# Even attention of a two-layer transformer: ScalarE's and VectorE's orders chained beside TensorE's, casts of keys dealt out one at a time, a second PSUM bank for filling products

## The chip, the cores and the metric

The program runs on one core of a Trainium2 chip. TensorE (PE) multiplies matrices into PSUM, ScalarE (ACT) and VectorE (DVE) work element by element and read PSUM, GpSimd (POOL) works on SBUF, SyncE (SP) starts transfers. Each engine takes its instructions in the order in which they stand and waits on semaphores for what another engine has to finish. The metric is the device time of one execution in microseconds (us), lower is better.

## The reference, cut to what matters

Two layers work on 512 tokens and 256 context tokens of width 1024, all in float32. The change touches the first ("even") layer's attention and what is computed beside it:

```python
u, v, q, k, vv = split(h @ w_in, ...)         # 512 + 512 + 512 + 512 + 512 columns
q, k = apply_rope(q, cos, sin), apply_rope(k, cos, sin)     # tokens only, not the context
k_all, v_all = concat([k, kc]), concat([vv, vvc])           # 768 keys
def diff_attn(q, k, v, lam):                  # 8 heads of 64, in 4 pairs; v: 4 x 128
    s = einsum('bqhd,bkhd->bhqk', q, k) * 64 ** -0.5
    p = softmax(s).reshape(b, 4, 2, tq, tk)
    return einsum('bhqk,bkhe->bqhe', p[:, :, 0] - lam * p[:, :, 1], v)
y = concat([chunk_mlp(u, v, w_s, b_s), rmsnorm(o, subln_g) * 0.8]) @ w_out
# chunk_mlp: gelu(u) * (w_s @ layernorm(gelu(v)) + b_s); the context's queries see the 256 context keys alone
```

## The kernel before, in words

Everything is held transposed, features on partitions. A float32 product is made of three products of rounded halves (`mm3`, L101 to L108): an operand is split by ScalarE's cast into a high half and by VectorE's or GpSimd's subtraction into a low half.

The attention (from L522) runs over four head pairs `t`, each with three query pairs `qp` of 2 x 128 queries (`qp` 0 and 1 are tokens with 768 keys, `qp` 2 is the context with 256 keys): 12 steps `n = 3t + qp`, and a 13th that finishes the last. A step scores its own queries and finishes those of the step before:

- `scores` ("00", "01", "10", "11": query block, head of the pair): four matmuls into a two-bank PSUM tile `pw` (two of them in all); VectorE's negated maximum (L567), ScalarE's exponential with the sum (L569). After the second head VectorE joins both, `e0 - lam * ratio * e1` (L575 to L579).
- `turned` ("t0" to "t2"): four transposes of joined tiles into a bank `pb` (three banks), ScalarE's cast and VectorE's subtraction split the result (`ath`, `atl`, L122 and L123).
- `weighed` ("a0" to "a2"): six matmuls with the values into a bank `pb` that is held over the whole step; ScalarE copies it out (L616).

`stack` (L534) makes for a pair and a head the operands of the scores: three casts by ScalarE (`qa`, twice `kh`: L539, L542, L543) and three subtractions by VectorE (L544, L546). The products of the 12 remaining column blocks of `w_in` (four of `q` and `k`, eight of `u` and `v`) are dealt in between as fillers of TensorE: `block` makes per column block four pieces of six 512-wide matmuls (tokens) and four pieces of six 256-wide ones (context); `fill_in` takes pieces from a queue by a clock of estimated times. All pieces go to one bank `pf`; ScalarE copies each half out (L641) before the next half may begin. The weights of a block come over a ring of six slots (three blocks); their casts are ScalarE's L81.

At the end of a step come the norm of a finished pair (its square by ScalarE L657, sums of the square over partitions by TensorE L156, a chain of small VectorE operations, spreads by TensorE L183), after step 8 four gelus (L674), and after steps 9 to 11 the turning of the gelu'd blocks with their statistics (`turn`). Behind the attention `mix` applies the layer norm (12 ScalarE operations L703, 12 of VectorE L705) and the chunk product; then comes the projection with `even_out`, whose weights are cast by ScalarE (L81, 128x1024) and completed by GpSimd.

What sets the order: a scheduler with an internal timeline places instructions on each engine, unless `tc.issue_after(x)` ties an instruction behind `x`. Before the change only TensorE's attention instructions are tied into a chain (`pe`, `tail`); those of ScalarE and VectorE stand where the scheduler put them.

## Time and profile before

| | us |
|---|---|
| median of 3 runs | 1615.69 (1614.0 to 1616.93) |
| profiled execution, its own time | 1613.23 |
| its span, first to last instruction | 1611.3 |
| mean granted TensorE clock | 0.982 |
| attention, first scores to the last filler | 130.6 to 351.9 |

Stretches are named by microseconds from the start of the span. In the views a row of waits reads: engine, tile and line that waited, what released it, total us, times, longest us. A row of a timeline reads: start, length, engine, line, operation, output and input tiles, count, and in brackets the idle time before it with its releaser. A row of stretches gives busy us and instructions of each engine, then the granted TensorE clock (PEclk, 1.00 is full), the busy share of the transfer engines and GB/s. In a row of grouped instructions, count, busy us and mean ns stand around the bar.

### The profile page before, as it was taken

To read this page: it belongs to the slowest core of one execution; us is meant where nothing else is said; L and a number is where in the kernel's file an instruction comes from. 1 tells how busy PE (TensorE), PEld (TensorE's weight loads), DVE (VectorE), ACT (ScalarE), POOL (GpSimd) and SP (SyncE) were. 2 spreads that over 40 slices of the span, in tenths; PEclk is the share of its full clock that TensorE was granted. 3 is DMA by queue.
4 is the path that set the end of the run, shared out by engine and by line. 5 is a ranking of instruction groups with operands and counts; after the bars stand their busy time and mean duration, and the time that the engine had idled before them with its cause. 6 is when DMAs were issued, how large, how long until landed. Compare 5 with 4: busy or idle time off the path is not lost.

```text
span 1611.3 us, 24978 instructions
## 1 busy us (share of the span) xinstructions
PE 1526.3 (95%) x9547; PEld 1358.2 (84%) x9547; DVE 1081.9 (67%) x1960; ACT 724.8 (45%) x1472; POOL 825.5 (51%) x563
## 2 busy tenths in 40 slices
PE   6998988979999999999999989999999999999996
PEld 4766877869998999999999978777869989999996
DVE  4517755654598787888896386666568976666656
ACT  2415555553463333333333334456556544454442
POOL 0442311023318677767776514641314399888883
PEclk9999999999999999999999999999999999999998
DMA  9770000024103333345543112210225233323301
GB/s 349 287 265 27 27 27 20 1 89 172 66 28 110 124 126 112 97 172 166 166 146 99 33 50 67 67 40 8 63 68 199 70 101 107 109 93 112 90 16 53
DMA packets 54295, 162.00 MB, mean 101 GB/s; under 512 B 6176, under 2 KB 10656, under 8 KB 46496
## 3 DMA queue, kind: packets, MB, share of 16 engines
q1 hardware_dynamic: 47120, 135.11, 25.0%
q10 hardware_dynamic: 7056, 25.30, 4.8%
q8 instruction: 75, 1.23, 0.3%
q14 instruction: 44, 0.36, 0.1%
HBM read 158.29 MB, written 2.10 MB: 100 GB/s over the span
## 4 chain that ended last, share of the span: by engine, by line
PE 78%; DVE 11%; issue 6%; ACT 3%; POOL 1%; DMA 1%; POOLq 0%; SPq 0%; DVEq 0%; ACTq 0%
PE pw L106 11%; PE pw L107 10%; PE pw L108 10%; PE pb L107 8%; PE pb L106 8%; PE pb L108 8%; PE pf L106 4%; PE pf L107 4%; PE pf L108 4%; PE pb L1526 2%; PE pb L1515 2%; PE pf L362 2%; PE pw L1478 1%; PE pw L1486 1%; DVE t L978 1%
## 5 line engine op out<-in xcount | busy, mean ns | idle before, releaser
L84 POOL TENSOR_TENSOR w<-raw,w 128x512 fp32r<-128x512 f32 (+1 forms) x86 | 127.9, 1493 | 258.7 <-ACT w L81 245.2
L873 DVE SCALAR_TENSOR_TENSOR xT<-pb,mod,xT 128x512 f32<-128x512 f32 (+3 forms) x208 | 145.7, 707 | 127.2 <-PE pb L108 126.9
L107 PE MATMUL pw<-ax,w 128*128 128x384 f32 (+2 forms) x708 | 225.2, 319 | 3.7 <-DVE ax L201 2.4
L106 PE MATMUL pw<-ax,w 128*128 128x384 f32 (+2 forms) x708 | 223.8, 320 | 4.6 <-DVE q L978 1.9
L108 PE MATMUL pw<-ax,w 128*128 128x384 f32 (+2 forms) x708 | 224.2, 318 | 0.1
L106 PE MATMUL pf<-ax,w 128*128 128x256 f32 (+2 forms) x484 | 167.7, 347 | 24.6 <-ACT f L641 19.2
L978 POOL TENSOR_TENSOR w<-raw,w 128x512 fp32r<-128x512 f32 x110 | 169.0, 1551 | 20.6 <-ACT w L978 20.5
L978 POOL TENSOR_TENSOR w<-t,w 128x512 fp32r<-128x512 f32 x99 | 148.8, 1506 | 56.2 <-ACT w L978 56.2
L106 PE MATMUL pb<-hh,w 128*128 128x512 f32 x480 | 171.2, 357 | 1.2 <-DVE xT L873 1.2
L108 PE MATMUL pb<-hh,w 128*128 128x512 f32 x480 | 171.5, 357 | 0.3 <-DVE w L978 0.3
L107 PE MATMUL pb<-hh,w 128*128 128x512 f32 x480 | 171.2, 357 | 0.0
L107 PE MATMUL pf<-ax,w 128*128 128x256 f32 (+2 forms) x484 | 163.1, 337 | 0.0
L108 PE MATMUL pf<-ax,w 128*128 128x256 f32 (+2 forms) x484 | 162.9, 337 | 0.0
L107 PE MATMUL pw<-T,w 128*128 128x384 f32 (+1 forms) x508 | 156.9, 310 | 1.2 <-DVE T L123 1.2
L106 PE MATMUL pw<-T,w 128*128 128x384 f32 (+1 forms) x508 | 156.3, 310 | 1.1 <-DVE hs L978 1.1
L108 PE MATMUL pw<-T,w 128*128 128x384 f32 (+1 forms) x508 | 157.0, 310 | 0.0
L107 PEld LDWEIGHTS pw<-ax,w 128*128 128x128 f32 x708 | 135.1, 191 | 9.8 <-DVE ax L201 3.6
L106 PEld LDWEIGHTS pw<-ax,w 128*128 128x128 f32 x708 | 134.3, 191 | 10.6 <-DVE q L978 2.6
L108 PEld LDWEIGHTS pw<-ax,w 128*128 128x128 f32 x708 | 135.3, 191 | 2.1 <-DVE w L1047 0.4
L978 POOL TENSOR_TENSOR hh<-hs,hh 128x768 fp32r<-128x768 f32 (+1 forms) x42 | 79.9, 1903 | 90.5 <-ACT hh L978 68.1
L106 PEld LDWEIGHTS pf<-ax,w 128*128 128x128 f32 x484 | 94.3, 195 | 35.3 <-ACT f L641 22.0
L978 POOL TENSOR_TENSOR w<-rawo,w 128x512 fp32r<-128x512 f32 x59 | 104.0, 1763 | 28.3 <-ACT w L978 28.3
(366 smaller groups left out, 3904.7 us busy)
## 6 DMA issues: line engine op xcount, KB each, us to landing
raw<-ffn_in SPq DMA_DIRECT2D x44, 1024.0 KB, 5.0
ar<-ada SPq DMA_DIRECT2D x24, 1024.0 KB, 6.9
ar<-ada ACTq DMA_DIRECT2D x48, 512.0 KB, 3.5
rawo<-ffn_out SPq DMA_DIRECT2D x88, 256.0 KB, 3.0
raw<-odd_out SPq DMA_DIRECT2D x32, 256.0 KB, 2.7
raw<-qk SPq DMA_DIRECT2D x16, 256.0 KB, 6.1
raw<-uv SPq DMA_DIRECT2D x16, 256.0 KB, 2.7
raw<-even_out SPq DMA_DIRECT2D x8, 512.0 KB, 3.9
```

The lines of the kernel that those rows point to most:

```text
L84: eng.tensor_tensor(lo, raw, hi.bitcast(F32), ALU.subtract)
L106: mm(out, s[0], m[0], start=start, stop=False, **kw)
L107: mm(out, s[0], m[1], start=False, stop=False, **kw)
L108: return mm(out, s[1], m[0], start=False, stop=stop, **kw)
L362: nc.tensor.matmul(ps[32 * q:32 * q + 32, :w], cst[:, k, :], t[:, w * q:w * q + w], start=k == 0, stop=k == KT - 1, skip_group_check=True)
L873: ins = self.nc.vector.scalar_tensor_tensor(h, ps[:, r], self.modcol(l, j, m, who), h, ALU.mult, ALU.add)
L978: tail[key] = fn(*args, **kw)
L1478: nc.tensor.matmul(ps[:, st:en], Q, K[g][p][:, b0 * P:b1 * P], start=p == 0, stop=p == 1, skip_group_check=True)
L1486: nc.tensor.matmul(ps[:, en:en + TC], Q, K[g][p][:, TX:], start=p == 0 and not edge, stop=p == 1, skip_group_check=True)
L1515: last = nc.tensor.transpose(pt[:, x * P:(x + 1) * P], es[2 * (x % 2) + x // 2][:, kb * P:(kb + 1) * P], self.ident)
L1526: nc.tensor.matmul(po[64 * h:64 * h + 64, :], V[vb][:, 64 * g:64 * g + 64], t[:, h * TC:h * TC + TC], start=kb == 0, stop=kb == nb - 1, sk ...
```

## The change

A helper `run` ties the attention's instructions into three chains, one per engine: an instruction of ScalarE or VectorE now stands in the order in which the program text names it. The joining of the two heads becomes a step of the plan ("c0", "c1"), the plans are rewritten, `stack` is cut into three portions (`keys(X)`, `queries`, `keys(Y)`, each one cast and one subtraction), which `spare` deals out after a "t" or "a"; what is left and the second head's three portions come in at "s". A filler's context half goes to one of the three banks `pb` in place of `pf`, and the rotation of a finished `q` or `k` block follows its token half. The casts of the fillers' weights, the gelus and the norms' squares are in ScalarE's chain too.

```diff
-        tail = []
-        def pe(fn, *args):
-            with tc.issue_after(tail[0].ins) if tail else ExitStack():
-                tail[:] = [fn(*args)]
+        tail, later = {}, []
+        def run(key, fn, *args, **kw):
+            with tc.issue_after(tail[key].ins) if key in tail else ExitStack():
+                tail[key] = fn(*args, **kw)
+            return tail[key]
+        pe = lambda fn, *args: run("PE", fn, *args)
+        act = lambda fn, *args, **kw: run("ACT", fn, *args, **kw)
+        dve = lambda fn, *args, **kw: run("DVE", fn, *args, **kw)
...
+            def queries():
+                act(nc.scalar.copy, m[X], q[X])
+                dve(nc.vector.tensor_tensor, m[Y], q[X], m[X].bitcast(F32), ALU.subtract)
+            def keys(Z):
+                act(nc.scalar.copy, kh[Z], k[X])
...
+                    dve(nc.vector.tensor_tensor, kl[Y], k[X], kh[X].bitcast(F32), ALU.subtract)
+            return [lambda: keys(X), queries, lambda: keys(Y)]
...
+        def joined(qb, st):
+            es, sums, eps = st["e"], st["sums"], st["eps"]
+            r = self.small(1, "sa", 10)
+            dve(nc.vector.reciprocal, r, sums[:, 1:2])
+            dve(nc.vector.scalar_tensor_tensor, r, r, self.nlam, sums[:, 0:1], ALU.mult, ALU.mult)
+            dve(nc.vector.scalar_tensor_tensor, es[0], es[1], r, es[0], ALU.mult, ALU.add)
...
             def load():
-                W.extend(self.blocks(a[name][n]))
+                with tc.issue_after(tail["ACT"].ins) if "ACT" in tail else ExitStack():
+                    W.extend(self.blocks(a[name][n]))
+                tail["ACT"] = self.last_cast
...
-                        box.append(self.fill()[:, :c.stop - c.start])
+                        box.append((self.bank if c.start else self.fill)()[:, :c.stop - c.start])
...
-                        nc.scalar.mul(u[:, c], box[0], scale)
-                        if done and c.start:
-                            done(u)
+                        act(nc.scalar.mul, u[:, c], box[0], scale)
+                        if done and not c.start:
+                            later.append(lambda: done(u))
...
-                nc.scalar.activation(sq, o, AF.Square)
+                act(nc.scalar.activation, sq, o, AF.Square)
...
         def gelu(i, after):
-            with tc.issue_after(after.ins):
-                return nc.scalar.activation(raw[i], raw[i], AF.Gelu)
+            return act(nc.scalar.activation, raw[i], raw[i], AF.Gelu)
...
-                        nc.scalar.activation(vg[:, s], vg[:, s], AF.Identity, bias=nb[:, t:t + 1], scale=rs[:, t:t + 1])
+                        act(nc.scalar.activation, vg[:, s], vg[:, s], AF.Identity, bias=nb[:, t:t + 1], scale=rs[:, t:t + 1])
...
+                if t < 3 and qp == 1:
+                    later += stack(t + 1, 0)
-            plan = "00 01 t0 t1 a0 t2 10 11 a1 a2" if long else "00 t0 a0 01 10 11"
+            plan = "00 t0 01 t1 c0 a0 t2 a1 10 11 s c1 a2" if long else "00 t0 01 c0 a0 10 11 c1"
...
+                elif v == "s":
+                    if cur and qp == 2 and t < 3:
+                        for fn in later + stack(t + 1, 1):
+                            fn()
+                        later.clear()
...
-                if t < 3 and qp == 1:
-                    stack(t + 1, 0)
-                if t < 3 and qp == 2:
-                    stack(t + 1, 1)
```

In the rows below the first name is what is written, behind the arrow what is read; L530 is the new helper's line. Place one is VectorE at the end of step 5, where the operands of the third head pair are made; `kl` and `qa` are the low halves of `stack`, the RECIPROCAL and the two rows behind it join the heads. Before:

```order
L567 TENSOR_REDUCE sa_1927<-pw_1924 128x1
L567 TENSOR_REDUCE sa_1927<-pw_1938 128x1
L546 TENSOR_TENSOR kl_1989<-f_157_1055,kh_1988 64x768 x2
L544 TENSOR_TENSOR qa_1986<-f_156_1054,qa_1986 64x768
L579 SCALAR_TENSOR_TENSOR sx_1505<-sa_1928 128x1
L544 TENSOR_TENSOR qa_2310<-f_158_1056,qa_2310 64x768
L546 TENSOR_TENSOR kl_2313<-f_159_1057,kh_2312 64x768 x2
L575 RECIPROCAL sa_1944<-sa_1928 128x1
L576 SCALAR_TENSOR_TENSOR sa_1944<-sa_1944,nlam,sa_1928 128x1
L577 SCALAR_TENSOR_TENSOR e_1930<-e_1942,sa_1944,e_1930 128x256
```

Place one, VectorE, now:

```order
L530 TENSOR_REDUCE sa_1939<-pw_1936 128x1
L530 TENSOR_REDUCE sa_1939<-pw_1944 128x1
L530 TENSOR_TENSOR kl_1969<-f_226_1345,kh_1968 64x768
L530 TENSOR_TENSOR qa_1967<-f_190_1170,qa_1967 64x768
L530 TENSOR_TENSOR kl_1969<-f_226_1345,kh_1968 64x768
L530 RECIPROCAL sa_1976<-sa_1940 128x1
L530 SCALAR_TENSOR_TENSOR sa_1976<-sa_1976,nlam,sa_1940 128x1
L530 SCALAR_TENSOR_TENSOR e_1942<-e_1948,sa_1976,e_1942 128x256
```

Three of the six subtractions between the last maximum and the joining have moved to earlier places; three are left. Place two is ScalarE in step 6: the square of the pair that step 5 finished (`sq`), among the exponentials (`e`) of step 6. Before:

```order
L569 ACTIVATE e_2005,sa_2003<-pw_1997,sa_2002 128x768
L122 CAST ath_2018<-pb_2013 128x512
L616 COPY o_1506<-pb_2028 128x256
L657 ACTIVATE sq_2098<-o_1506 128x768
L569 ACTIVATE e_2042,sa_2003<-pw_2036,sa_2002 128x768
L641 ACTIVATE f_161_1059<-pf_1972 128x512
L569 ACTIVATE e_2064,sa_2062<-pw_2056,sa_2061 128x768
L81 CAST w_2140<-raw_2138 128x512
L569 ACTIVATE e_2079,sa_2062<-pw_2073,sa_2061 128x768
```

Place two, ScalarE, now:

```order
L530 ACTIVATE e_1998,sa_1996<-pw_1990,sa_1995 128x768
L530 CAST ath_2011<-pb_2006 128x512
L530 ACTIVATE e_2027,sa_1996<-pw_2021,sa_1995 128x768
L530 COPY o_1496<-pb_2034 128x256
L530 ACTIVATE f_381_2048<-pf_1960 128x512
L530 ACTIVATE e_2058,sa_2056<-pw_2050,sa_2055 128x768
L530 ACTIVATE e_2073,sa_2056<-pw_2067,sa_2055 128x768
L530 ACTIVATE sq_2092<-o_1496 128x768
```

The square has moved behind all four exponentials of the step. Place three is ScalarE at the end: `f` are the blocks of `u` and `v` (copied out of `pf` or `pb`, normalised with `sf`, gelu'd), `ax` the high halves of the projection's operands, `w` the high halves of its weights. Before:

```order
L703 ACTIVATE f_162_1060<-f_162_1060,sf_3161,sf_3149 128x128 x3
L703 ACTIVATE f_163_1061<-f_163_1061,sf_3161,sf_3149 128x128 x3
L641 ACTIVATE f_166_1064<-pf_2966 128x256
L674 ACTIVATE f_166_1064<-f_166_1064 128x768
L641 ACTIVATE f_167_1065<-pf_3033 128x512
L122 CAST ax_3227<-o_1105 128x768
L122 CAST ax_3231<-o_1506 128x768
L122 CAST ax_3235<-o_1996 128x768
L641 ACTIVATE f_167_1065<-pf_3090 128x256
L674 ACTIVATE f_167_1065<-f_167_1065 128x768
L81 CAST w_3138<-raw_3139 128x1024
```

Place three, ScalarE, now:

```order
L530 ACTIVATE f_584_3088<-pb_3090 128x256
L530 ACTIVATE f_341_1866<-f_341_1866,sf_3161,sf_3149 128x128 x3
L530 ACTIVATE f_381_2048<-f_381_2048,sf_3161,sf_3149 128x128 x3
L530 ACTIVATE f_420_2222<-f_420_2222,sf_3161,sf_3149 128x128 x3
L530 ACTIVATE f_453_2382<-f_453_2382,sf_3161,sf_3149 128x128 x3
L530 ACT_TABLE_LOAD
L530 ACTIVATE f_473_2499<-f_473_2499 128x768
L530 ACTIVATE f_524_2740<-f_524_2740 128x768
L530 ACTIVATE f_560_2937<-f_560_2937 128x768
L530 ACTIVATE f_584_3088<-f_584_3088 128x768
L81 CAST w_3138<-raw_3139 128x1024
```

Between the copy of the last filler and the first weight cast of the projection stood one gelu; now twelve normalisations, a table load and four gelus stand there.

More of the change, by code (lines that the diff above doesn't have):

```diff
@@ L251, in rope @@
         nc.vector.stream_shuffle(sh, ps, ROT)
-        nc.vector.tensor_tensor(out, ps, tabs[0], ALU.mult)
+        self.last_rope = nc.vector.tensor_tensor(out, ps, tabs[0], ALU.mult)
         nc.gpsimd.tensor_tensor(sh, sh, tabs[1], ALU.mult)
@@ L538, in stack @@
             m = Ra.tile([P, TA], F32R, name=self.uid("qa"), tag="sq", bufs=3)
-            nc.scalar.copy(m[X], q[X])
             kh = Ra.tile([P, TA], F32R, name=self.uid("kh"), tag="sk", bufs=6)
             kl = Ra.tile([P, TA], F32R, name=self.uid("kl"), tag="sk", bufs=6)
-            nc.scalar.copy(kh[X], k[X])
-            nc.scalar.copy(kh[Y], k[X])
-            nc.vector.tensor_tensor(m[Y], q[X], m[X].bitcast(F32), ALU.subtract)
-            for Z in (X, Y):
-                nc.vector.tensor_tensor(kl[Z], k[X], kh[X].bitcast(F32), ALU.subtract)
-            QK[t][0][c], QK[t][1][c] = m, (kh, kl)
+            QK[t][0][c], QK[t][1][c] = m, (kh, kl)
+            def queries():
[3 more added lines that the diff above has]
+                act(nc.scalar.copy, kh[Z], k[X])
+                if Z == X:
+                    dve(nc.vector.tensor_tensor, kl[X], k[X], kh[X].bitcast(F32), ALU.subtract)
+                else:
+                    dve(nc.vector.tensor_tensor, kl[Y], k[X], kh[X].bitcast(F32), ALU.subtract)
+            return [lambda: keys(X), queries, lambda: keys(Y)]
         def scores(t, qb, c, st):
@@ L566, in scores @@
             nm, sums = st["nm"], st["sums"]
-            nc.vector.tensor_reduce(nm[:, c:c + 1], ps[:, koff:TA], axis=AX, op=ALU.max, negate=True)
+            dve(nc.vector.tensor_reduce, nm[:, c:c + 1], ps[:, koff:TA], axis=AX, op=ALU.max, negate=True)
             e = Ra.tile([P, TA], F32, name=self.uid("e"), tag="e", bufs=5)
-            self.last_exp = nc.scalar.activation(e[:, koff:], ps[:, koff:TA], AF.Exp, bias=nm[:, c:c + 1],
-                                                 accum_out=sums[:, c:c + 1])
-            es = st["e"]
-            es.append(e[:, koff:])
-            if c:
-                r = self.small(1, "sa", 10)
-                nc.vector.reciprocal(r, sums[:, 1:2])
-                nc.vector.scalar_tensor_tensor(r, r, self.nlam, sums[:, 0:1], ALU.mult, ALU.mult)
-                nc.vector.scalar_tensor_tensor(es[0], es[1], r, es[0], ALU.mult, ALU.add)
-                eps = st["eps"]
-                nc.vector.scalar_tensor_tensor(eps[:, qb:qb + 1], sums[:, 0:1], EPS, sums[:, 0:1], ALU.mult, ALU.mult)
+            self.last_exp = act(nc.scalar.activation, e[:, koff:], ps[:, koff:TA], AF.Exp, bias=nm[:, c:c + 1],
+                                accum_out=sums[:, c:c + 1])
+            st["e"].append(e[:, koff:])
+        def joined(qb, st):
[4 more added lines that the diff above has]
+            dve(nc.vector.scalar_tensor_tensor, es[0], es[1], r, es[0], ALU.mult, ALU.add)
+            dve(nc.vector.scalar_tensor_tensor, eps[:, qb:qb + 1], sums[:, 0:1], EPS, sums[:, 0:1], ALU.mult, ALU.mult)
         def turned(pair, i):
@@ L594, in turned @@
             tl = Ra.tile([P, 512], F32R, name=self.uid("atl"), tag="at", bufs=6)
-            self.split(th, tl, pt)
+            act(nc.scalar.copy, th, pt)
+            dve(nc.vector.tensor_tensor, tl, pt, th.bitcast(F32), ALU.subtract)
             pair["at"][i] = th, tl
@@ L615, in weighed @@
             if i == n - 1:
-                nc.scalar.copy(pair["o"][:, qp * TC:(qp + 1) * TC], po)
+                act(nc.scalar.copy, pair["o"][:, qp * TC:(qp + 1) * TC], po)
         def block(name, n, out, scale, done=None):
@@ L628, in piece @@
                 return ins
-            u = f3()
-            out[1][out[0]] = u
             todo = []
@@ L637, in step @@
                     if k0 == 0:
-                        box.append(self.fill()[:, :c.stop - c.start])
+                        box.append((self.bank if c.start else self.fill)()[:, :c.stop - c.start])
                     pe(piece, box[0], A, k0)
                     if k0 == KT - 2:
-                        nc.scalar.mul(u[:, c], box[0], scale)
-                        if done and c.start:
-                            done(u)
+                        if not c.start:
+                            out[1][out[0]] = f3()
+                        u = out[1][out[0]]
+                        act(nc.scalar.mul, u[:, c], box[0], scale)
+                        if done and not c.start:
+                            later.append(lambda: done(u))
                 todo += [(us, lambda k0=k0, step=step: step(k0)) for k0 in range(0, KT, 2)]
@@ L660, in norm @@
                 sq = norms[t][2]
-                with tc.issue_after(tail[0].ins):
+                with tc.issue_after(tail["PE"].ins), tc.issue_after(tail["DVE"].ins):
                     norms[t] = o, eps, self.rstd_diag([(sq[:, :TX], TX), (sq[:, TX:], TC)], 1.0 / P, eps=eps)
-                tail[:] = [self.last_sum]
+                tail["PE"], tail["DVE"] = self.last_sum, self.last_diag
             else:
@@ L666, in norm @@
                     c = o[:, off:off + T]
-                    with tc.issue_after(tail[0].ins):
+                    with tc.issue_after(tail["PE"].ins):
                         r = self.spread(dg)
-                    tail[:] = [self.last_spread]
-                    nc.vector.scalar_tensor_tensor(c, c, self.subg, r, ALU.mult, ALU.mult)
+                    tail["PE"] = self.last_spread
+                    dve(nc.vector.scalar_tensor_tensor, c, c, self.subg, r, ALU.mult, ALU.mult)
         def gelu(i, after):
-            with tc.issue_after(after.ins):
-                return nc.scalar.activation(raw[i], raw[i], AF.Gelu)
+            return act(nc.scalar.activation, raw[i], raw[i], AF.Gelu)
         halves = ((0, 4), (4, 2))
@@ L684, in turn @@
                 ps = self.bank()
-                with tc.issue_after(tail[0].ins):
-                    for i in range(n):
-                        ins = nc.tensor.transpose(ps[:, i * P:(i + 1) * P], vg[:, (off + i) * P:(off + i + 1) * P], self.ident)
-                tail[:] = [ins]
-                nc.scalar.copy(vg[:, off * P:(off + n) * P], ps[:, :n * P])
-                for i in range(n):
-                    t = g * 6 + off + i
-                    nc.vector.bn_stats(stats[:, t, :], ps[:, i * P:(i + 1) * P])
-                    nc.vector.bn_aggr(mv[:, t, :], stats[:, t, :])
+                for i in range(n):
+                    pe(nc.tensor.transpose, ps[:, i * P:(i + 1) * P], vg[:, (off + i) * P:(off + i + 1) * P], self.ident)
+                act(nc.scalar.copy, vg[:, off * P:(off + n) * P], ps[:, :n * P])
+                for i in range(n):
+                    dve(nc.vector.bn_stats, stats[:, g * 6 + off + i, :], ps[:, i * P:(i + 1) * P])
+                for i in range(n):
+                    dve(nc.vector.bn_aggr, mv[:, g * 6 + off + i, :], stats[:, g * 6 + off + i, :])
         def mix(g, rs):
@@ L709, in mix, with turn_em @@
                                         sgub[:, g * P:(g + 1) * P].unsqueeze(1).to_broadcast([P, n, P]), ALU.add)
-        turn_em = lambda u: self.rope(u[:, :TX], u[:, :TX], tabs)
+        def turn_em(u):
+            with tc.issue_after(tail["DVE"].ins):
+                self.rope(u[:, :TX], u[:, :TX], tabs)
+            tail["DVE"] = self.last_rope
         fillers = [block("qk1", n, (key, qk), 0.125 if key < 4 else 1.0, turn_em) for n, key in enumerate((2, 6, 3, 7))]
@@ L730, in fill_in, with spare @@
                 clock[1] += d
+        def spare(n=1):
+            for _ in range(n):
+                if later:
+                    later.pop(0)()
         ahead(2)
-        stack(0, 0)
-        stack(0, 1)
-        epss, os, prev, last_gelu = {}, {}, None, None
+        for v in stack(0, 0) + stack(0, 1):
+            v()
+        epss, os, prev = {}, {}, None
         for n in range(13):
@@ L749, in even @@
                         fill_in(0.35 if v[0] == "t" else 0.71)
+                elif v == "s":
[3 more added lines that the diff above has]
+                        later.clear()
+                elif cur and v[0] == "c":
+                    joined(2 * qp + int(v[1]), cur["b"][int(v[1])])
                 elif cur:
                     i, c = int(v[0]), int(v[1])
-                    with tc.issue_after(last_gelu.ins) if last_gelu else ExitStack():
-                        scores(t, 2 * qp + i, c, cur["b"][i])
+                    scores(t, 2 * qp + i, c, cur["b"][i])
                     fill_in(0.7 if qp < 2 else 0.24)
+                if v[0] in "at":
+                    spare()
             if prev and prev["qp"] == 2:
@@ L769, in even @@
                     for i in (4, 5, 6, 7):
-                        last_gelu = gelu(i, self.last_exp)
+                        gelu(i, None)
                     fill_in(3.0)
```

## The prediction

> **What bounds the kernel now.** I read the page's engine line first, then TensorE's waits in the attention, then the rows around the longest ones, then the clock by stretches.

> ```profile
> PE 1526.3 (95%) x9547; PEld 1358.2 (84%) x9547; DVE 1081.9 (67%) x1960; ACT 724.8 (45%) x1472; POOL 825.5 (51%) x563
> PE pf L106 <- ACT f L641: 19.2, 10, 4.9
> ...
> PE pb L107 <- DVE atl L123: 3.1, 5, 1.3
> ```

> TensorE is the bound, and in the attention (130 to 353 us) it waits most for the copy that empties the single bank `pf`; five waits for a split tile (`atl`) are short. What is taken off its path in the attention moves the end, and the rest of the program follows unchanged behind it. The longest waits one by one, and a shorter one to compare:

> ```profile
> 178.95 0.72 PE L588 MATMUL pb<-ident,e 128*128 128x128 f32 x3 [2.56 <-DVE e L577]
> 224.66 0.79 PE L106 MATMUL pf<-ax,w 128*128 128x512 f32 x1 [4.48 <-ACT f L641]
> 276.62 0.79 PE L106 MATMUL pf<-ax,w 128*128 128x512 f32 x1 [3.98 <-ACT f L641]
> 327.08 0.39 PE L106 MATMUL pf<-ax,w 128*128 128x256 f32 x1 [1.94 <-ACT f L641]
> 339.12 0.80 PE L106 MATMUL pf<-ax,w 128*128 128x512 f32 x1 [4.91 <-ACT f L641]
> ```

> The first three stand where one head pair gives way to the next. ScalarE says why: after the last score it works through casts for the next pairs, and the copy that frees `pf` stands behind them.

> ```profile
> 218.31 0.83 ACT L542 CAST kh<-f 64x768 fp32r<-64x768 f32 x1
> ...
> 224.23 0.38 ACT L641 ACTIVATE f<-pf 128x256 f32<-128x256 f32 x1
> ```

> Each of the four long waits is followed by half clock; the wait of 1.94 us lies in a stretch at full clock:

> ```profile
> 179.20:182.60 3.40, 3.40 (x12) 2.83 (x11) 0.85 (x2) 0.99 (x3) 0.00 (x0) 0.50 0.00 0
> 223.60:230.40 6.80, 5.74 (x18) 4.87 (x19) 3.54 (x6) 1.86 (x6) 1.32 (x1) 0.50 0.11 39
> 274.80:281.60 6.80, 4.99 (x12) 3.92 (x13) 0.00 (x0) 3.01 (x6) 2.51 (x2) 0.50 0.00 0
> 281.60:336.20 54.60, 46.46 (x294) 39.88 (x292) 35.78 (x133) 30.09 (x63) 2.59 (x2) 1.00 0.05 14
> 336.20:343.00 6.80, 3.88 (x9) 3.10 (x10) 0.92 (x4) 3.72 (x9) 0.00 (x0) 0.50 0.78 280
> ```

> TensorE is busy for 3.40 + 5.74 + 4.99 + 3.88 = 18.0 us at clock 0.50, which full clock would do in half: 9.0 us lost, 2.25 per drop.

> **The change, part by part.** The unit prices, first TensorE's from successive starts, then the others' means:

> ```profile
> 244.78 0.40 PE L559 MATMUL pw<-kh,qa 128*128 128x512 f32 x1
> 245.48 0.40 PE L106 MATMUL pf<-ax,w 128*128 128x512 f32 x1
> 246.88 0.40 PE L559 MATMUL pw<-kh,qa 128*128 128x512 f32 x1
> 249.78 0.36 PE L106 MATMUL pb<-ath,vhi 128*128 128x256 f32 x1
> 250.57 0.39 PE L106 MATMUL pf<-ax,w 128*128 128x512 f32 x1
> ```

> A score of 768 keys takes 0.70, a filler piece of 512 columns 1.40, a weighing 0.79.

> ```profile
> L81 ACT CAST w<-raw 128x512 fp32r<-128x512 f32 x18 | 11.1, 616 | 2.5 <-PE pf L108 2.1 <-issue 0.2
> L569 ACT ACTIVATE e<-pw,sa 128x256 f32<-128x256 f32 x16 | 7.6, 476 | 9.3 <-DVE sa L567 9.1
> L542 ACT CAST kh<-f 64x768 fp32r<-64x768 f32 x8 | 6.6, 830 | 0.1
> L674 ACT ACTIVATE f<-f 128x768 f32<-128x768 f32 x8 | 6.4, 837 | 0.1
> L703 ACT ACTIVATE f<-f,sf,sf 128x128 f32<-128x128 f32 x12 | 4.7, 478 | 0.7 <-DVE sf L798 0.7
> L674 ACT ACT_TABLE_LOAD x2 | 2.6, 1283 | 0.0
> L546 DVE TENSOR_TENSOR kl<-f,kh 64x768 fp32r<-64x768 f32 x16 | 15.9, 991 | 1.1 <-ACT kh L542 0.9
> L544 DVE TENSOR_TENSOR qa<-f,qa 64x768 fp32r<-64x768 f32 x8 | 7.6, 950 | 0.1
> L577 DVE SCALAR_TENSOR_TENSOR e<-e,sa,e 128x256 f32<-128x256 f32 x8 | 4.8, 598 | 0.2
> ```

> *Number of instructions.* The same casts, subtractions, matmuls and weight transfers are issued; SP's order stays, and on POOL one weight subtraction changes places with its neighbour. That costs nothing by itself; only the places count.

> *Turns from one pair to the next.* Before: 2.56 + 4.48 + 3.98 = 11.0 us. Now the context half is written to `pb`, so the next block's `pf` is long free; late next is the joined tile that "t0" transposes. From step 5 to step 6 TensorE has, after the last score, a filler (1.40), a weighing (0.79), a score (0.70) and a filler (1.40) = 4.3 us. Against it stand the exponential's end, about 1.2 us after the score (two maxima and two exponentials of 256 columns, of which the 0.476 of the row is one), two weight casts (2 x 0.62, which now stand in ScalarE's chain between the exponential and the first key cast), that cast (0.83), three subtractions on VectorE (2 x 0.99 + 0.95) and the joining (0.6, and some 0.4 for its two small operations) = 7.2 us: a wait of 2.9. The next weighing waits about 0.8 more, since maximum, exponential, cast and subtraction all stand behind the joining. So 3.7 in place of 4.48. From step 2 to 3 no weight cast stands there: 2.5. From step 8 to 9 the joining has cover. But ScalarE now has three casts of `stack` (2.5), a table load (1.28), four gelus (3.35), two weight casts (1.23) and another table load (1.28) ahead of step 9's first exponential (0.9), and the split of the first turned tile (about 1.3) behind that: 11.8 us. TensorE has four filler pieces (5.6), two scores (1.4), two context pieces (1.4, half as wide) and four transposes (about 0.4) = 8.8, so the first weighing waits 3. Sum 9.2, a gain of 1.8.

> *Squares.* Before, each stood ahead of the step's exponentials, and the sums over it (L156) did not wait. Now it is behind the last one. The starts of the sums and of that exponential before, in steps 3, 6 and 9:

> ```profile
> 188.43 1.50 PE L156 MATMUL pb<-ones,sq 128*128 128x128 f32 x12
> 189.59 0.92 ACT L569 ACTIVATE e<-pw,sa 128x768 f32<-128x768 f32 x1
> ...
> 240.59 1.50 PE L156 MATMUL pb<-ones,sq 128*128 128x128 f32 x12
> 240.60 0.90 ACT L569 ACTIVATE e<-pw,sa 128x768 f32<-128x768 f32 x1
> ...
> 293.79 1.50 PE L156 MATMUL pb<-ones,sq 128*128 128x128 f32 x12
> 293.61 0.90 ACT L569 ACTIVATE e<-pw,sa 128x768 f32<-128x768 f32 x1
> L657 ACT ACTIVATE sq<-o 128x768 f32<-128x768 f32 x4 | 3.4, 846 | 0.1
> ```

> With the exponential holding ScalarE for 0.8 us and the square for 0.85, the sums of step 6 can begin at 242.3, 1.7 late; in step 3 a context copy (0.38) lies between: 191.6, 3.2 late; in step 9 two weight casts: 296.5, 2.7 late. That is 7.6 us of new waits. TensorE has nothing else there: the sums are the next in its chain.

> *The end.* Before, the last filler's matmul ends at 351.88, the first weight cast follows one gelu later, and the projection starts at 355.32:

> ```profile
> 351.60 0.28 PE L108 MATMUL pf<-ax,w 128*128 128x256 f32 x1
> 353.09 1.98 ACT L81 CAST w<-raw 128x1024 fp32r<-128x1024 f32 x2
> 355.32 0.43 PE L106 MATMUL pw<-ax,w 128*128 128x384 f32 x1
> ```

> That is 3.4 us. Now the cast stands behind the last copy (0.4), twelve normalisations (4.7), a table load (1.28) and four gelus (3.35) and takes 1.0 itself: 10.8 us. TensorE meanwhile has the spreads and some of the chunk product, both of which it did before too. Cost 7.4 us, and nothing behind it gives that back, since TensorE is at 95% of the span.

> *The rest.* The other eight waits for `pf` (19.2 - 4.48 - 3.98 = 10.7 us, 4.91 among them) go. What comes instead no row shows: three banks now hold a weighing, a context filler and the transposed tiles, so a "t" may wait until the tile before it is split, and VectorE's joining stands ahead of the maxima. The nearest row is that of the waits for `atl`, mean 0.6 and longest 1.3 us. The bounds: no such wait (a gain of 10.7), and the longest in each of twelve steps (15.6, a loss of 5). I take 0.9 a step, between mean and longest, since every step now has the crowded banks: 10.8, and the item comes to 0.

> *Clock.* Waits of 2.5 us and more lowered it, 1.94 did not. By the above five new ones are that long (turns at 3.7 and 3, squares at 3.2 and 2.7, the end), 5 x 2.25 = 11.3 against 9.0: 2.3 lost. [...]

> *Sum.* -1.8 + 7.6 + 7.4 + 0 + 2.3 = +15.5 us. The profiled execution took 1613.2 us (span 1611.3 and 1.9 around it), so 1628.7; the median of the runs is 2.5 us above it: 1631.2.

> **The rivals.** *The bank pays in full and the clock stays up (faster).* Nothing replaces the other waits for `pf` (-10.7), the weight casts are not in the way at step 6 (turns -3.0), and only the end costs clock (2.25 - 9.0 = -6.8); squares and end stay (+15.0). Sum -5.5: 1610. It decides where rest and clock together save more than the 13.2 us that squares and end, less the turns' 1.8, cost. For it speaks that ScalarE is busy only 45% of the span; against it that the new waits are of order, not of load.

> *VectorE's fixed order holds TensorE in every step.* Rest at its upper bound (+5), about 1.4 us more in each of the three squares' steps, since a joining now precedes the last two maxima (+4), and nine drops of the clock (+11). With turns, squares and end: +33, 1649. For it speaks that VectorE is busy 39.7 of 54.7 us in a pair's time:

> ```profile
> 174.00:228.70 54.70, 45.93 (x267) 39.90 (x266) 39.72 (x83) 28.12 (x57) 13.72 (x10) 0.92 0.09 29
> ```

> *A wait costs clock only where it fills a window of 3.4 us.* Then two drops are left (step 6 and the end), 4.5 - 9.0 = -4.5 in place of +2.3: +8.7, 1624. The drops in the trace last 3.4 or 6.8 us, which speaks for such a window; the drop after 2.56 us of waiting speaks against it. [...]

> *It changes nothing in sum:* waits change their names and places, 1616. The end speaks against it.

> **How the numbers follow.** A measurement of this kernel can tell about 0.2% (3.2 us) from no change. Forecast (1622 to 1641 by itself) 0.40; faster rival 0.25; VectorE's order 0.15; clock by window 0.15; no change 0.05. So faster 0.25, same 0.05, slower 0.70. The range runs from inside the faster rival, 1604, to just under the upper one, 1648.

> **What would show it.** Right: TensorE's waits for the copy (L641's successor) gone; waits of the sums for `sq` in steps 3, 6, 9 of 2 to 4 us each; the transposes of steps 3 and 6 waiting 2 to 3 us for the joined `e`; some 10 us between the last filler and the first product of the projection, with the clock at 0.50 after it. Wrong: if those sums start without a wait, if few stretches at 0.50 are left between 130 and 345 us, or if the projection starts within 5 us of the last filler.

## The result and the profile after

The changed kernel takes 1624.0 us (median of 4 runs, 1623.6 to 1626.8), the kernel before in the same series 1614.9: a ratio of 1.0058, 95% interval 1.0041 to 1.0076. It is slower, by 9.1 us. The profiled execution took 1624.4 us with a span of 1622.3, 11.0 longer than that of before.

The page's engine line, TensorE again the busiest:

```profile
PE 1529.9 (94%) x9547; PEld 1361.7 (84%) x9547; DVE 1092.1 (67%) x1960; ACT 719.8 (44%) x1472; POOL 824.8 (51%) x563
```

TensorE's waits from 128 to 378 us, the attention and the start of the projection:

```profile
PE pb L601 <- DVE e L530: 8.7, 4, 3.8
PE pb L156 <- ACT sq L530: 7.8, 3, 3.8
PE pb L106 <- ACT ath L530: 6.1, 6, 2.2
PE pf L720 <- DVE f L721: 3.8, 4, 1.7
PE pb L601 <- DVE atl L530: 3.2, 3, 2.1
```

No wait for a copy out of `pf` is left, where 19.2 us stood before. In their place TensorE waits for joined tiles, for squares, and for split tiles.

Where the 11.0 us lie is read from stretches with the same bounds in both programs. First before, then after: from the 100th us to the end of the last filler, and from there to a point in the projection from which the two profiles run at an equal distance.

```profile
100.00:351.88 251.88, 218.43 (x1256) 180.46 (x1255) 149.16 (x371) 127.87 (x250) 43.07 (x32) 0.94 0.15 51
351.88:384.00 32.12, 30.47 (x186) 29.00 (x185) 16.37 (x17) 15.11 (x17) 25.08 (x10) 1.00 0.25 83
```

```profile
100.64:358.14 257.50, 219.22 (x1257) 181.77 (x1256) 155.12 (x371) 115.64 (x234) 43.19 (x32) 0.95 0.15 50
358.14:394.94 36.80, 32.36 (x185) 30.88 (x185) 19.86 (x19) 24.17 (x34) 24.71 (x10) 0.95 0.35 112
```

The first stretch is 5.6 us longer (257.50 less 251.88), the second 4.7; 0.6 lie ahead of them, and the 1227 us behind them differ by 0.1. TensorE's idle time (length less busy) is 33.4 and then 38.3 us in the first, 1.7 and then 4.4 in the second. Of its busy time 23.8 us were at clock 0.50 before and 28.8 after, half of which is counted as lost: 11.9 and 14.4. That is an estimate from the clock; in the changed kernel's timeline 512-wide filler products start 0.43 us apart at 0.50 (from 195.34 to 197.90) and 0.23 at full clock (from 229.06 to 230.20), so the loss is a little under half.

The waits that the prediction named, in TensorE's timeline after (steps 3, 6 and 9):

```profile
181.22 0.33 PE L601 MATMUL pb<-ident,e 128*128 128x128 f32 x1 [1.74 <-DVE e L530]
...
193.27 0.38 PE L156 MATMUL pb<-ones,sq 128*128 128x128 f32 x1 [3.80 <-ACT sq L530]
...
237.34 0.47 PE L601 MATMUL pb<-ident,e 128*128 128x128 f32 x1 [3.83 <-DVE e L530]
...
249.36 0.38 PE L156 MATMUL pb<-ones,sq 128*128 128x128 f32 x1 [1.50 <-ACT sq L530]
...
295.02 0.38 PE L106 MATMUL pb<-ath,vhi 128*128 128x256 f32 x1 [2.19 <-ACT ath L530]
...
304.80 0.38 PE L156 MATMUL pb<-ones,sq 128*128 128x128 f32 x1 [2.47 <-ACT sq L530]
```

The turns cost 1.7 + 3.8 + 2.2 = 7.8 us in place of 11.0, the sums wait 7.8 for squares. ScalarE's timeline at the end, and TensorE's last filler product, the chunk products (L720) and the first product of the projection:

```profile
358.45 4.72 ACT L530 ACTIVATE f<-f,sf,sf 128x128 f32<-128x128 f32 x12
363.17 1.28 ACT L530 ACT_TABLE_LOAD   x1
364.46 3.04 ACT L530 ACTIVATE f<-f 128x768 f32<-128x768 f32 x4
367.42 2.92 ACT L81 CAST w<-raw 128x1024 fp32r<-128x1024 f32 x3
```

```profile
357.86 0.28 PE L108 MATMUL pb<-ax,w 128*128 128x256 f32 x1
357.97 0.38 PE L720 MATMUL pf<-sguT,f 128*128 128x128 f32 x2
...
366.69 1.16 PE L720 MATMUL pf<-sguT,f 128*128 128x128 f32 x8 [1.71 <-DVE f L721]
368.50 0.64 PE L106 MATMUL pw<-ax,w 128*128 128x384 f32 x1 [0.65 <-ACT w L81]
```

From the last filler's end at 358.1 to the projection are 10.4 us, before 3.4. One more row proved to be the one that matters: ScalarE's largest wait between 130 and 345 us, before and after.

```profile
ACT e L569 <- DVE sa L567: 37.5, 20, 4.4
```

```profile
ACT e L530 <- DVE sa L530: 87.4, 36, 6.7
```

ScalarE stands 87.4 us, not 37.5, in front of an exponential whose maximum VectorE has not delivered, and everything that its chain puts behind that exponential stands too. The rows under e11 show it at one place: ScalarE stands idle for 2.57 us up to 167.23, although the transposes that its next cast reads end at 166.02 (165.47 and 0.55).

### The profile page after: what moved, and what is told of

Same layout as the page of the kernel before. It is cut to its first block, busy times and chain, and to the rows that moved or that the text cites. A ratio compares the mean times of both kernels' runs of the same rounds, so it can differ in the third digit from the quotient of the medians.

```text
span 1622.3 us, 24975 instructions
## 1 busy us (share of the span) xinstructions
PE 1529.9 (94%) x9547; PEld 1361.7 (84%) x9547; DVE 1092.1 (67%) x1960; ACT 719.8 (44%) x1472; POOL 824.8 (51%) x563
## 3 DMA queue, kind: packets, MB, share of 16 engines
q1 hardware_dynamic: 47120, 135.11, 24.8%
q8 instruction: 75, 1.23, 0.3%
## 4 chain that ended last, share of the span: by engine, by line
PE 78%; DVE 13%; ACT 6%; issue 2%; POOL 0%; DMA 0%; ACTq 0%; POOLq 0%; SPq 0%; DVEq 0%
PE pw L106 11%; PE pw L107 11%; PE pw L108 11%; PE pb L107 8%; PE pb L106 8%; PE pb L108 8%; PE pf L106 3%; PE pf L107 3%; PE pf L108 3%; PE pb L1556 2%; PE pb L1545 2%; ACT e L530 2%; DVE sa L530 2%; PE pf L362 2%; PE pw L1508 1%
## 5 line engine op out<-in xcount | busy, mean ns | idle before, releaser
L106 PE MATMUL pw<-ax,w 128*128 128x384 f32 (+2 forms) x708 | 224.5, 321 | 4.7 <-DVE q L1008 1.9
L107 PE MATMUL pw<-ax,w 128*128 128x384 f32 (+2 forms) x708 | 225.5, 319 | 2.7 <-DVE ax L465 1.4
L108 PE MATMUL pw<-ax,w 128*128 128x384 f32 (+2 forms) x708 | 224.3, 318 | 0.1
L106 PE MATMUL pb<-hh,w 128*128 128x512 f32 x480 | 171.0, 356 | 1.2 <-DVE xT L903 1.2
L108 PE MATMUL pb<-hh,w 128*128 128x512 f32 x480 | 171.6, 357 | 0.3 <-DVE w L1008 0.3
L107 PE MATMUL pb<-hh,w 128*128 128x512 f32 x480 | 171.2, 357 | 0.0
L107 PE MATMUL pw<-T,w 128*128 128x384 f32 (+1 forms) x508 | 157.0, 310 | 1.2 <-DVE T L123 1.2
L106 PE MATMUL pw<-T,w 128*128 128x384 f32 (+1 forms) x508 | 156.3, 310 | 1.1 <-DVE hs L1008 1.1
L108 PE MATMUL pw<-T,w 128*128 128x384 f32 (+1 forms) x508 | 157.1, 310 | 0.0
L106 PEld LDWEIGHTS pw<-ax,w 128*128 128x128 f32 x708 | 134.5, 191 | 10.7 <-DVE q L1008 2.6
L107 PEld LDWEIGHTS pw<-ax,w 128*128 128x128 f32 x708 | 135.1, 191 | 8.8 <-DVE ax L201 2.8
L106 PE MATMUL pf<-ax,w 128*128 128x512 f32 (+2 forms) x388 | 136.7, 352 | 5.7 <-DVE qf L252 5.7
L108 PEld LDWEIGHTS pw<-ax,w 128*128 128x128 f32 x708 | 134.8, 191 | 2.2 <-DVE w L1077 0.4
L108 PE MATMUL pf<-ax,w 128*128 128x512 f32 (+2 forms) x388 | 134.3, 346 | 0.0
L107 PE MATMUL pf<-ax,w 128*128 128x512 f32 (+2 forms) x388 | 134.1, 346 | 0.0
L228 DVE SCALAR_TENSOR_TENSOR junk<-ar,cb 128x1024 bf16<-128x1024 f32 x64 | 106.8, 1668 | 0.0
```

The lines of the kernel that those rows point to most:

```text
L106: mm(out, s[0], m[0], start=start, stop=False, **kw)
L107: mm(out, s[0], m[1], start=False, stop=False, **kw)
L108: return mm(out, s[1], m[0], start=False, stop=stop, **kw)
L228: return self.nc.vector.scalar_tensor_tensor(junk, t, 1.0, self.cb[who], ALU.mult, ALU.mult, accum_out=self.acc[who][:, col:col + 1])
```

## The experiments

Twelve kernels were run in three series, each series with the kernel before on the same chip. Ratios are to the kernel before in that series; its median was 1613.6 to 1615.0 us, so medians of different series can differ by 1.4 us for that alone. The last three columns are of the one profiled execution: the length of the attention stretch of the section above (from the 100th us to the end of the last filler, with the start moved to the same instruction), and TensorE's idle time and clock loss from the 100th us to one and the same instruction of the projection, which lies a little ahead of the end of the second stretch above.

| kernel | median us | ratio, 95% interval | attention us | idle us | clock loss us |
|---|---|---|---|---|---|
| before (first series) | 1614.9 | 1 | 251.9 | 34.8 | 11.9 |
| changed | 1624.0 | 1.0058, 1.0041 to 1.0076 | 257.5 | 42.7 | 14.4 |
| e1, second bank alone | 1596.3 | 0.9900, 0.9885 to 0.9915 | 231.0 | 23.3 | 3.2 |
| e2, changed, one bank | 1633.0 | 1.0118, 1.0098 to 1.0138 | 265.4 | 45.2 | 18.5 |
| e3, changed, squares early | 1625.5 | 1.0072, 1.0055 to 1.0089 | 255.1 | 40.9 | 13.6 |
| e4, changed, end free | 1621.2 | 1.0054, 1.0037 to 1.0072 | 260.3 | 42.4 | 12.7 |
| e5, changed, VectorE free | 1619.1 | 1.0025, 1.0013 to 1.0036 | 246.0 | 35.8 | 13.0 |
| e6, changed, ScalarE free | 1592.8 | 0.9866, 0.9849 to 0.9883 | 232.3 | 23.3 | 6.6 |
| e7, changed, both free | 1605.4 | 0.9938, 0.9919 to 0.9957 | 237.8 | 28.2 | 7.3 |
| e8, e1 and keys dealt out | 1600.9 | 0.9911, 0.9896 to 0.9926 | 234.9 | 23.8 | 8.0 |
| e9, changed, fillers' work free | 1614.5 | 1.0006, 0.9997 to 1.0015 | 251.7 | 35.4 | 10.4 |
| e10, changed, splits free | 1610.5 | 0.9975, 0.9965 to 0.9986 | 246.7 | 35.2 | 12.4 |
| e11, changed, exponentials free | 1600.7 | 0.9917, 0.9902 to 0.9932 | 232.3 | 24.8 | 9.1 |
| e12, e6, last gelus late | 1594.0 | 0.9877, 0.9864 to 0.9889 | 230.2 | 20.9 | 6.4 |

### e1: the second bank alone

The kernel before with one edit:

```diff
-                        box.append(self.fill()[:, :c.stop - c.start])
+                        box.append((self.bank if c.start else self.fill)()[:, :c.stop - c.start])
```

> The kernel before with one edit of the change: the context half of each filling block uses one of the three small banks in place of pf's. Theory (the waits for the copy out of pf are real, and three small banks suffice as long as ScalarE and VectorE are free to take work out of order): of the 19.2 us of waits for the copy under 3 are left, TensorE's idle time up to the last filler falls from 33.4 to about 22 us, the stretches at half clock cost about 7 in place of 11.9 us; about 1601 to 1605 us. Rival (the crowded small banks give one wait for each that goes): idle time 31 to 36 us, 1612 to 1618 us.

Measured: 1596.3 us, 17 less than before and 5 below the theory's range. The idle time fell by 11.5 us and the clock loss by 8.7. TensorE's largest waits:

```profile
PE pb L588 <- DVE e L577: 7.0, 3, 3.1
PE pb L107 <- DVE atl L123: 1.9, 5, 0.5
```

The copy is gone from the list, and no crowding of the three small banks has come in its place: all waits for VectorE's half of a split tile (`atl`) come to 5.2 us in eight, where before there were 3.1 in five, and those for the joined tile to 7.0, where before there were 3.8; together far less than the 19.2 us that went. So the rest of the change, its written orders and its plan, costs 26 us (by the ratios) to 28 (by the medians) against this kernel.

### e2: the changed kernel with one bank

```diff
-                        box.append((self.bank if c.start else self.fill)()[:, :c.stop - c.start])
+                        box.append(self.fill()[:, :c.stop - c.start])
```

> The changed kernel with both halves of a filling block in pf again, its order kept. Theory (the bank pays about what the waits for the copy were worth outside the turns, 10.7 us, and the rest of the new order pays nothing): 8 to 12 us slower than the changed kernel, 1632 to 1636 us, with waits for the copy of 10 us or more. Rival (the written order of the scores already spaces the copies so that one bank is enough): within 3 us of the changed kernel.

Measured: 1633.0 us, 9 slower than the changed kernel. TensorE waits for the copy again:

```profile
PE pf L106 <- ACT f L530: 16.7, 10, 4.1
```

The bank pays 9 us here and 17 in the old order; the written order does not do its work for it.

### e3: the squares early

```diff
+                        if v == "a0" and prev["qp"] == 2:
+                            norms[prev["t"]] = os[prev["t"]], epss[prev["t"]]
+                            norm(prev["t"], 0)
...
-            if prev and prev["qp"] == 2:
-                norms[prev["t"]] = os[prev["t"]], epss[prev["t"]]
-                norm(prev["t"], 0)
```

> The changed kernel with one edit: in steps 3, 6 and 9 the square stands in ScalarE's chain right behind the copy of the context block, ahead of the last two exponentials, as it did before. Theory: the sums' waits (7.8 us in the changed kernel) go, with one stretch at half clock behind them (about 1.5 us): 1613 to 1617 us. Rival (the two exponentials are then late by the square's 0.85 us, and the joining, the transposes of the next step and the turn wait instead): 4 us or more of the 7.8 come back under these names, 1619 to 1623 us.

Measured: 1625.5 us, not faster (the intervals of the two ratios overlap). The 7.8 us of waits for `sq` are gone from the profile, and TensorE waits longer elsewhere:

```profile
PE pb L106 <- ACT ath L530: 8.2, 5, 3.0
PE pb L530 <- DVE mv L530: 4.3, 1, 4.3
PE pb L601 <- DVE atl L530: 4.0, 4, 1.9
```

Split tiles took 6.1 and 3.2 us before this edit, the statistics 2.0. In all TensorE's idle time fell by 1.8 us (42.7 to 40.9), so 6.0 of the 7.8 came back, and the rival holds in its waits: TensorE got to the next thing that ScalarE's chain had not reached. Its time of 1619 to 1623 us did not come. The attention stretch is 2.4 us shorter, but the part of the program behind, which is the same in both, took longer in this execution. The squares were the place of most of these waits, not their cause.

### e4: the end free

```diff
-                        act(nc.scalar.activation, vg[:, s], vg[:, s], AF.Identity, bias=nb[:, t:t + 1], scale=rs[:, t:t + 1])
+                        nc.scalar.activation(vg[:, s], vg[:, s], AF.Identity, bias=nb[:, t:t + 1], scale=rs[:, t:t + 1])
...
-                gelu(k, self.last_exp)
+                with tc.issue_after(self.last_exp.ins):
+                    nc.scalar.activation(raw[k], raw[k], AF.Gelu)
```

> The changed kernel with one edit: the twelve normalisations on ScalarE and the gelus of the blocks 0 to 3 at the end are out of ScalarE's chain, as before. Theory (ScalarE's order causes the end's loss): from the end of the last filler to the first product of the projection 3 to 5 us in place of 10.4; the changed kernel lost 5.0 us between these and the common pace of the projection, and 4 to 5 of these come back: 1619 to 1620 us. Rival (the first weight cast waits for the room of the weights or for the load, not for ScalarE): 10 us stay, 1623 to 1625 us.

Measured: 1621.2 us, 2.9 less by the medians and 0.6 by the ratios. The intervals overlap, so no gain is shown. In TensorE's timeline the projection starts 3.8 us after the last filler (360.2 to 363.99), as the theory said; but free gelus and their table load now stand ahead of the copies of the last turned block, and the last step's transposes wait for its bank, 3.94 us where the changed kernel has 1.47:

```profile
343.11 1.09 PE L601 MATMUL pb<-ident,e 128*128 128x128 f32 x4 [3.94 <-DVE mv L530]
...
363.99 0.42 PE L106 MATMUL pw<-ax,w 128*128 128x384 f32 x1
```

So ScalarE's order makes the late start of the projection. The attention stretch, though, became 2.8 us longer, most of it this one wait, which gave back a part of what the end cost.

### e5, e6 and e7: without VectorE's chain, without ScalarE's, without both

```diff
# e5 (and the ties that name tail["DVE"] left out)
-        dve = lambda fn, *args, **kw: run("DVE", fn, *args, **kw)
+        dve = lambda fn, *args, **kw: fn(*args, **kw)
# e6 (the weights' casts untied too; gelus and scores tied to each other as before); e7 has both
-        act = lambda fn, *args, **kw: run("ACT", fn, *args, **kw)
+        act = lambda fn, *args, **kw: fn(*args, **kw)
```

> The changed kernel without VectorE's chain (ScalarE's and TensorE's stay). The second bank alone gave 1596 us, so the rest of the change costs 28 us; this run and the next two ask which part. Theory S (ScalarE's chain: waits of the sums for the square 7.8, of the weighings for the cast tile 6.1, the end 5, and half clock behind them): within 4 us of the changed kernel, 1620 to 1626. Theory V (VectorE's chain holds the joining and the split tiles): 1600 to 1612 us. Theory P (TensorE's new plan): within 4 us of the changed kernel.

> The changed kernel without ScalarE's chain (the gelus are tied to the exponentials as before; VectorE's and TensorE's chains stay). Theory S: waits for the square and for the cast tile under 3 us together, 1600 to 1608 us. Theory V: 1618 to 1626 us, waits for the joined tile stay at 8 us or more. Theory P: 1614 us or more, the waits change their names.

> The changed kernel with neither ScalarE's nor VectorE's chain; the new plan of TensorE, the keys dealt out singly and the second bank stay. Theory S or V: near the second bank alone, 1595 to 1602 us. Theory P: 1612 us or more.

Measured: 1619.1, 1592.8 and 1605.4 us. ScalarE's chain costs 31 us, and without it this is the fastest kernel of the study, 1.3% faster than before. Theory S holds in e6, by more than its range; theories V and P are out as the main cause: VectorE's chain costs 5 us while ScalarE is chained, and it saves 13 once ScalarE is free (e7 against e6, intervals apart). In the attention stretch e5 is 11.5 us shorter than the changed kernel; behind it, where the program is the same, its profiled execution lost about half of that again, and why was not settled. e7 lies between the bounds that were set for it: the new plan without either chain is 6 us (by the ratios) to 9 (by the medians) slower than the second bank alone, and what of it makes that was not settled. ScalarE's largest waits and TensorE's in e6:

```profile
ACT ath L534 <- PE pb L601: 28.3, 20, 3.2
ACT e L534 <- DVE sa L530: 23.2, 17, 5.9
```

```profile
PE pw L571 <- ACT e L534: 4.0, 3, 2.3
PE pb L601 <- DVE mv L530: 3.9, 1, 3.9
PE pb L530 <- DVE mv L530: 3.4, 1, 3.4
PE pb L601 <- DVE e L530: 3.1, 2, 1.8
```

ScalarE now waits mostly for TensorE, which is the right way round, and its waits for maxima fell from 87.4 to 23.2 us. In e7 TensorE waits 8.3 us for joined tiles, in e6 3.1: there VectorE's fixed order helps.

### e8: the second bank and the keys dealt out

The kernel before with the edit of e1, and `stack` cut into the three portions of the change; those of the first head follow one at a time after a "t" or an "a" of the step ahead.

```diff
+                if t < 3 and qp == 1:
+                    later += stack(t + 1, 0)
...
+                    if later:
+                        later.pop(0)()
```

> The kernel before with the second bank and the first head's casts of queries and keys dealt out singly over the step ahead, nothing chained and TensorE's old plan. Theory (the turns' waits for the joined tile, 7.0 us in the second bank alone, come from the six casts and six subtractions in a heap): 4 us of them go, 1590 to 1594 us. Rival (the scheduler had them spread already, or the dealt ones now stand ahead of maxima and exponentials): 1595 to 1600 us.

Measured: 1600.9 us, no gain over the bank alone (intervals overlap). Waits for the joined tile stay at 7.1 us: the rival holds (its upper end was 1600), dealing the casts out buys nothing where the scheduler places them.

### e9, e10 and e11: what in ScalarE's chain holds it up

```diff
# e9: fillers' copies and weight casts out of the chain (the weights' tie left out too)
-                        act(nc.scalar.mul, u[:, c], box[0], scale)
+                        nc.scalar.mul(u[:, c], box[0], scale)
# e10: splits of turned tiles out
-            act(nc.scalar.copy, th, pt)
+            nc.scalar.copy(th, pt)
# e11: exponentials out (gelus and scores tied to each other as before)
-            self.last_exp = act(nc.scalar.activation, e[:, koff:], ps[:, koff:TA], AF.Exp, bias=nm[:, c:c + 1],
+            self.last_exp = nc.scalar.activation(e[:, koff:], ps[:, koff:TA], AF.Exp, bias=nm[:, c:c + 1],
```

> The changed kernel with the fillers' work on ScalarE (the copies out of pf and pb, the casts of their weights) out of the chain; the attention's own ScalarE work, the squares and the end stay in it. Freeing the whole chain gave 31 us (1624.0 to 1592.8). Theory F (the fillers' copies and weight casts stand among the attention's and hold them up, or are held up): more than half of it, 1594 to 1608 us. Theory H (an exponential that waits for VectorE's maximum holds up what stands behind it, splits of turned tiles and squares): under 10 us, 1615 to 1624 us.

> The changed kernel with ScalarE's half of the split of the turned tiles (ath) out of the chain, all else in it. Theory H: the 6.1 us of waits of the weighings for ath and a part of what VectorE's half (atl) and the joining wait for go, with the half clock behind them: 1606 to 1616 us. Theory F: 1618 to 1625 us.

> The changed kernel with the exponentials out of ScalarE's chain (the gelus are tied to them as before), all else in it, splits, squares and fillers' copies among them. Theory H: splits and copies pass the exponentials that wait; 10 us or more of the 31 come back, 1600 to 1614 us. Theory F: under 8 us, 1616 to 1625 us.

Measured: 1614.5, 1610.5 and 1600.7 us, so 9.5, 13.5 and 23.3 us of the 31 (they overlap: their sum is more than the whole). Freeing the exponentials alone, with squares, splits, copies and casts still in their written order, gives three quarters of it; that is theory H. The fillers' work gives less than F asked for and lies at the edge of what H allowed.

The attention stretch shows it more sharply. First e11, then e6, against 257.50 us in the changed kernel:

```profile
101.35:333.68 232.33, 211.94 (x1257) 177.09 (x1256) 153.59 (x371) 116.87 (x234) 43.56 (x32) 0.96 0.16 56
```

```profile
101.45:333.74 232.29, 210.56 (x1257) 176.29 (x1256) 152.01 (x371) 126.66 (x250) 43.27 (x32) 0.96 0.16 55
```

Freeing the exponentials gives 25.2 us there, as much as freeing all of ScalarE's work; what e11 lacks to e6 lies at the end, where its projection still starts 10.4 us after the last filler. Freeing the fillers' work gives 5.8 us there; the rest of its gain is at the end, where with the copies free the projection starts 3.8 us after the last filler. In e11 ScalarE's wait for maxima has shrunk, and TensorE's for squares too, though the squares stayed in ScalarE's chain:

```profile
ACT e L581 <- DVE sa L530: 24.4, 16, 4.9
```

```profile
PE pb L601 <- DVE e L530: 4.9, 5, 1.8
...
PE pb L156 <- ACT sq L530: 1.4, 2, 1.2
```

The mechanism at one place, the first turned tile in step 2. The changed kernel, TensorE's transposes and next weighing, and then ScalarE's rows:

```profile
165.47 0.55 PE L601 MATMUL pb<-ident,e 128*128 128x128 f32 x3 [1.78 <-DVE e L530]
...
169.05 0.39 PE L106 MATMUL pb<-ath,vhi 128*128 128x256 f32 x1 [0.94 <-DVE atl L530]
```

```profile
167.23 0.47 ACT L530 ACTIVATE e<-pw,sa 128x256 f32<-128x256 f32 x1 [2.57 <-DVE sa L530]
...
167.70 0.58 ACT L530 CAST ath<-pb 128x512 fp32r<-128x512 f32 x1
```

And the same place in e11, ScalarE, where the transposes start at 163.83:

```profile
164.42 0.59 ACT L530 CAST ath<-pb 128x512 fp32r<-128x512 f32 x1 [1.39 <-PE pb L601]
165.59 0.47 ACT L581 ACTIVATE e<-pw,sa 128x256 f32<-128x256 f32 x1 [0.58 <-DVE sa L530]
```

The exponential begins 1.76 us after the first of these transposes in both. The split begins 2.23 us after it in the changed kernel and 0.59 in e11: there ScalarE, idle either way, takes it while VectorE is still at the maximum, and the weighing has no wait.

### e12: e6 with the last gelus late

```diff
-                gelu(k, self.last_exp)
+                with tc.issue_after(self.last_o.ins):
+                    gelu(k, self.last_exp)
```

> The kernel of the earlier run without ScalarE's chain (1592.8 us), with one tie more: the gelus of the blocks 0 to 3 stand behind the last weighing's copy. In that run a table load and two gelus stand ahead of the last turned block's copies, and the last step's transposes wait 3.9 us for the bank that these empty. Theory: 2 to 3 us of that wait go, and with it one stretch at half clock: 1588 to 1591 us. Rival (the gelus are then late for the projection): 1592 to 1596 us.

Measured: 1594.0 us, no gain (intervals overlap). `last_o` is the last weighing's copy. The wait of 3.9 us shrank to 1.5 as expected and the attention stretch by 2.1, but the time did not follow. Between the attention and the last 15 us of the program the profile of e12 has four stretches at half clock, that of e6 two, though the program there is the same; the last section shows what such a stretch depends on.

## Why the prediction was right and wrong

The sign came out and the time lay in the range; the size was 7 us too high (1631.2 against 1624.0), one term was mis-sized, and the cause behind another was wrong.

- **Turns.** Predicted 9.2 us in place of 11.0 (2.5, 3.7, 3.0), measured 7.8 (1.7, 3.8, 2.2). The path named for step 6 (weight casts, key cast, three subtractions, joining) is the one in the trace, but that 3.7 and 3.8 agree is luck: the transposes were to wait 2.9 and waited 3.8, since the first subtraction took 2.02 us in place of 0.99, and the 0.8 put down to the next weighing did not come.
- **Squares.** Predicted 7.6, measured 7.8 (3.8, 1.5, 2.5). The wait was foreseen, its price was not: with the squares early most of it came back as other waits (e3).
- **The end.** The step that failed in size: "Cost 7.4, and nothing behind it gives that back". The projection did start late by 7.0 us (10.4 less 3.4). But TensorE did 32 of the 48 chunk products in that time where before it had done 12, products that it otherwise does later at full cost. The stretch grew by 4.7 us, of which 1.7 are clock that the sum counts apart: 3.0 in place of 7.4.
- **The rest.** Predicted 0, measured +0.3 (idle time to the last filler less turns and squares: 22.4 and 22.7). The size fits by chance. The step said that crowded banks would bring back the 10.7 us that the copies no longer take. They do not: in e1 the same three banks take the context fillers and 17 us are gained. What brought them back, and more, is ScalarE's chain (e6, e11). The row for it was in the profile before, 37.5 us of ScalarE's waits for maxima; the prediction did not weigh it and looked only at ScalarE's busy share, 45% of the span.
- **Clock.** Predicted +2.3 us, measured +2.5 (14.4 less 11.9), and that too is luck. Of the five waits named, four are followed by half clock (the square's in step 9, 2.47 us, is not), three other stretches at half clock came (from 146.7, 208.1 and 344.7), and the first one in the attention is half as long as before. The rule behind the term, that a wait of some 2.5 us lowers the clock, is not the right one (below).
- **Median against profile.** The 2.5 us added to come from the profiled execution to the median were scatter: the 23 runs of before beside e9 to e12 took 1610.7 to 1617.5. Without them the forecast was 1628.7, and the profiled execution took 1624.4; the end's 4.4 us alone make up the 4.3 between, and the other errors cancel.

The rival "the bank pays in full and the clock stays up" described e1, and the half of it that failed was the assumption that squares and end are all that the written order costs. Of "VectorE's fixed order holds TensorE in every step" the engine was wrong: freeing VectorE alone gave 5 us, freeing ScalarE alone 31. The rival in which a wait costs clock only where it fills a window gave 1624, the measured time, by luck: it had the clock 4.5 us better than before, and it was 2.5 worse; the end and the turns, which it priced too high, made up for most of that. No run shows that a wait has to fill such a window: in all but one of 107 windows more than 1.9 us of idle time was enough (below).

## What to carry to other kernels

An order written out for an engine that waits often makes each of its waits a wait for all that stands behind (here the exponentials' place alone was worth 23.3 of 31 us): look at how long the engine already waits for one input (here 37.5 us for maxima), and assume that more work will stand in that line, even on an engine that is idle half the time. Test the parts of such a change alone: here one line, a second bank, was worth 1.0%, and the rest of the change hid it. A wait that one moves away is priced only by a run, since the next one in the same chain may take its place (in e3 6.0 of 7.8 us came back).

## What the runs showed of the hardware

```profile
191.08:194.49 3.41, 1.22 (x10) 1.22 (x11) 1.52 (x6) 3.17 (x8) 0.69 (x1) 1.00 0.01 2
194.49:197.90 3.41, 3.41 (x12) 2.73 (x10) 2.58 (x11) 0.00 (x0) 1.81 (x2) 0.50 0.37 109
204.73:208.14 3.41, 1.34 (x12) 1.14 (x11) 1.36 (x3) 3.07 (x6) 0.00 (x0) 1.00 0.00 0
208.14:211.55 3.41, 3.41 (x18) 3.41 (x17) 3.28 (x7) 1.02 (x2) 0.00 (x0) 0.50 0.00 0
300.31:303.72 3.41, 2.02 (x10) 1.36 (x8) 1.59 (x4) 2.74 (x7) 0.15 (x1) 1.00 0.01 2
303.72:307.13 3.41, 2.33 (x16) 2.20 (x17) 2.65 (x7) 1.03 (x2) 3.13 (x2) 1.00 0.00 0
307.13:310.54 3.41, 1.76 (x13) 1.34 (x12) 3.14 (x18) 1.35 (x3) 0.00 (x0) 1.00 0.00 0
```

The wait of 2.07 us that ends at 207.78 lies inside one window, which leaves 1.34 us busy: half clock follows. The longer wait of 2.47 us that ends at 304.80 is cut by the border at 303.72 into 1.39 and 1.08 and costs no clock. A window did not have to stand idle as a whole: the one from 204.73 to 208.14 was idle for 2.07 of its 3.41 us. The windows' place against the program differs between the profiled executions (a window begins 0.5 to 3.2 us after the same instruction near the 100th us), and runs of one program differ with their clock: of e7's six runs the fastest took 1600.3 us at a mean clock of 0.986, the slowest 1609.2 at 0.978. That the place of the windows makes this scatter is argued, not shown.
